# The low-part scores matmul over 128 rows instead of 64, with the low part of k kept twice per head

## The chip, the cores and the metric

The kernel runs on one core of one Trainium2 chip. The metric is the device time of one execution in microseconds (us), from the first to the last instruction of that core. Timed runs are given as a median; the profile is of one separate execution of the same program.

## The reference

Two layers of a block that mixes a latent sequence of 256 tokens with a context of 256 tokens, both of width 1024, all in float32. Each layer has a feed-forward part, a mixer, and a second feed-forward part; the last layer leaves out what only the context would need. The mixer is the part that matters here. It projects to queries, keys and values of 64 per head, and computes

```
s = jnp.einsum('bqhgd,bkhd->bhgqk', qi, k).astype(jnp.float32) * scale
p = jax.nn.softmax(s, axis=-1).astype(v.dtype)
return jnp.einsum('bhgqk,bkhd->bqhgd', p, v)
```

for attention A (6 query heads on 2 key heads, with normed q and k, and rotary positions for the latent tokens) and attention B (6 heads, with a position bias and a window for the latent tokens). Latent queries see 256 latent and 256 context keys, context queries the 256 context keys alone. A short convolution over 256 channels is the third mixer, and the three results are projected by w_o. Width of a head: 64, half of the 128 rows of TensorE's array.

## The kernel before

**Numbers.** Float32 products are made of three matmuls of the type float32r: an operand x is split into a high part h (x cast to float32r) and a low part l = x - h, and x times w is h*wh + l*wh + h*wl. Weights come by DMA into a staging buffer (stg, two of them), ScalarE casts the high part (L93), VectorE subtracts to get the low one (L94), and both stand in one buffer of a ring of eight (name w, each 128x2x1024). All matmuls go through one helper (L79).

**Scores.** Since a head has 64 rows, high and low part of q share one stationary block of 128 rows: for the head of half b (rows R[b], 0 to 63 or 64 to 127), the rows R[b] of the block hold the high part, the other 64 the low one. That is AQ for attention A and BQ for B. The keys' high part stands in both halves (AK, BK), so that one matmul over 128 rows gives qh*kh + ql*kh. The low part of k stands once, in the rows of its own head (AL 128x512 for two heads, BL likewise), so the second matmul runs over 64 rows only, those of qh, and gives qh*kl. `unit` does this for a head and 128 queries:

```
mm(ps, q, k, True, False)
mm(ps, q[R[b]], kl[R[b]], False, True)
```

Behind it come, per unit: VectorE's negative row maximum nmx (L571; with bias, the sum and maximum in one, L574), ScalarE's exponential P with its row sum (L579), VectorE's reciprocal and scaling (L581, L582), two or four transpositions on TensorE (ptr, L586), ScalarE's copy PT (L588). `pair` takes two units (b = 0, 1) and multiplies their PT with V (pv, a stationary block of 64 columns each). The scores take one of two PSUM banks (name at).

**Stages.** `mixer` runs once per layer. In layer 0 (`full`) it has latent and context queries: 24 units of 256 keys and 24 of 512. In layer 1 it has the latent ones alone: 24 units of 512. So there are 72 units. `token_block` projects V, q and k of 128 tokens and fills AQ, AK and AL through a transposition (L471 to L480); `fm_b` projects q and k of attention B and fills BK, BQ and BL (L527 to L533), which lie in ring buffers, four of the eight, until attention B is done; `fm_conv` is the convolution, with six weight units. The output projection needs eight weight units (woa).

**Order.** The code above is traced in program order, and a scheduler then orders each engine's instructions by a model of its own. So ordinary matmuls of the projections and of the output projection stand between the scores, transpositions and pv of the attention. Each engine works its instructions in that order. SyncE's queue issues the DMAs of weights (stg) and of the bias (L606, two bias buffers in layer 0, four in layer 1) in order too: one that waits for its buffer holds up those behind it.

Of the kernel before, what the change touches and what calls it, by code (L numbers as in the profile page):

```python
# [8 lines left out]
F32 = mybir.dt.float32  # L9
F32R = mybir.dt.float32r  # L10
BF16 = mybir.dt.bfloat16
AF = mybir.ActivationFunctionType
ALU = mybir.AluOpType
# [12 lines left out]
def tile_hybrid_block(ctx: ExitStack, tc: tile.TileContext, xin, c2, w_ada, w_ada0, bcol, grow, gcol, win, qkg, bias_in,  # L26
                      convw, woa, wi, wi_tm, wo, ident, rope, out):
    nc = tc.nc
    pe, act, dve, pool, sp = nc.tensor, nc.scalar, nc.vector, nc.gpsimd, nc.sync
# [17 lines left out]
    CW = const.tile([128, 2, 3, 2], F32, name="CW")  # L47
# [30 lines left out]
    def mm(out, lhsT, rhs, first, last):  # L78
        pe.matmul(out, lhsT=lhsT, rhs=rhs, start=first, stop=last)  # L79
# [341 lines left out]
    def mixer(ph, l, U, after):  # L421
# [8 lines left out]
        nq = 512 if full else 256  # L430
        AQ = ph.tile([128, 3, 2, nq], F32R, name="AQ", tag="AQ")
        AK = ph.tile([128, 2, 512], F32R, name="AK", tag="AK")
        AL = ph.tile([128, 512], F32R, name="AL", tag="AL")
        R = [slice(0, 64), slice(64, 128)]

        wv = [load_unit(win[l, j]) for j in range(4)]
# [1 line left out]
        BQ, BK, BL = [], [], []  # L438

        def token_block(t):  # L440
            p = tm_block(U, t, wv)
            act.copy(V[:, t], p)
            h0 = 0 if (full or t < 2) else 6
            nh = 8 - h0
            p = tm_block(U, t, wqk, 64 * h0)
            pv = p.rearrange("p (h d) -> p h d", d=64)[:, h0:8]
            sq = ph.tile([128, 8, 64], F32, name="sq", tag="t2", bufs=4)
            act.activation(sq[:, h0:8], pv, AF.Square)
            ss = small.tile([128, 8], F32, name="ss8", tag="ss8")
            dve.tensor_reduce(out=ss[:, 0:nh], in_=sq[:, h0:8], op=ALU.add, axis=AX.X)  # L450
            r = rstd(ss[:, 0:nh], 64, nh)
            qn = ph.tile([128, 8, 64], F32, name="qn", tag="t2", bufs=4)
            dve.tensor_tensor(out=qn[:, h0:8], in0=pv, in1=r.unsqueeze(2).to_broadcast([128, nh, 64]), op=ALU.mult)
            dve.tensor_tensor(out=qn[:, h0:8], in0=qn[:, h0:8], in1=GT[:, h0:8], op=ALU.mult)
            if t < 2:
                m1 = ph.tile([128, 8, 64], F32, name="m1", tag="t2", bufs=4)
                dve.tensor_tensor(out=m1, in0=qn, in1=ROPE[:, t, 0:1].to_broadcast([128, 8, 64]), op=ALU.mult)
                m2 = sq
                qv = qn.rearrange("p h (a s f) -> p (h a) s f", a=2, s=2)
                mv = m2.rearrange("p h (a s f) -> p (h a) s f", a=2, s=2)  # L460
                sv = ROPE[:, t, 1].rearrange("p (a s f) -> p a s f", a=2, s=2)
                for s in range(2):
                    dve.tensor_tensor(
                        out=mv[:, :, s].rearrange("p (h a) f -> p h a f", a=2),
                        in0=qv[:, :, 1 - s].rearrange("p (h a) f -> p h a f", a=2),
                        in1=sv[:, :, s].unsqueeze(1).to_broadcast([128, 8, 2, 16]), op=ALU.mult)
                dve.tensor_tensor(out=qn, in0=m1, in1=m2, op=ALU.add)
            pt = ps_tr.tile([128, 4, 128], F32, name="ptr", tag="ptr")
            j0 = h0 // 2
            for j in range(j0, 4):  # L470
                pe.transpose(pt[:, j], qn[:, 2 * j:2 * j + 2].rearrange("p h d -> p (h d)"), I)  # L471
            c = slice(128 * t, 128 * t + 128)
            for b in range(2):
                if j0 == 0:
                    act.copy(AQ[R[b], :, b, c], pt[R[b], 0:3])
                    dve.tensor_tensor(out=AQ[R[1 - b], :, b, c], in0=pt[R[b], 0:3],
                                      in1=AQ[R[b], :, b, c].bitcast(F32), op=ALU.subtract)
                act.copy(AK[R[b], b, c], pt[R[b], 3])
                dve.tensor_copy(AK[R[1 - b], b, c], AK[R[b], b, c])
                dve.tensor_tensor(out=AL[R[b], c], in0=pt[R[b], 3], in1=AK[R[b], b, c].bitcast(F32), op=ALU.subtract)  # L480

        def fm_tile(idx, c0, n, w=None):
            w = w or load_unit(win[l, idx])
# [7 lines left out]
            return p  # L491

        oa = work.tile([128, 2, 512], F32, name="uf", tag="uf")
        ob = ph.tile([128, 512], F32, name="ob", tag="ob")
        oc = work.tile([128, 2, 512], F32, name="xn", tag="xn")
        od = work.tile([128, 4, 256], F32, name="grow", tag="grow")
        b0 = 256 if full else 0
# [15 lines left out]
        def fm_b():  # L513
            ws = {8 + x: load_unit(win[l, 8 + x]) for x in (0, 3, 1, 4)}
            bl = []
            for _ in range(4):
                w = next_slot().rearrange("p a (b c) -> p (a b) c", c=512)
                dve.memset(w[0:1, 0, 0:1].bitcast(F32), 0.0)
                bl.extend(w[:, x] for x in range(4))
            for j in range(3):  # L520
                BK.append(bl[2 * j:2 * j + 2])
                BQ.append(bl[6 + 2 * j:8 + 2 * j])
                BL.append(bl[12 + j])
            for j in range(3):
                p = fm_tile(8 + j, 0, 512, ws.get(8 + j))
                for b in range(2):
                    act.copy(BK[j][b][R[b]], p[R[b]])  # L527
                    dve.tensor_copy(BK[j][b][R[1 - b]], BK[j][b][R[b]])
                    dve.tensor_tensor(out=BL[j][R[b]], in0=p[R[b]], in1=BK[j][b][R[b]].bitcast(F32), op=ALU.subtract)
                p = fm_tile(11 + j, 0, nq, ws.get(11 + j))  # L530
                for b in range(2):
                    act.activation(BQ[j][b][R[b], 0:nq], p[R[b], 0:nq], AF.Copy, scale=0.125)
                    dve.scalar_tensor_tensor(out=BQ[j][b][R[1 - b], 0:nq], in0=p[R[b], 0:nq], scalar=0.125,  # L533
                                             in1=BQ[j][b][R[b], 0:nq].bitcast(F32), op0=ALU.mult, op1=ALU.subtract)

        def fm_conv():
            for ct in range(2):
                px = fm_tile(14 + 3 * ct, 0, nq)
                cx = ph.tile([128, 512], F32, name="cx", tag="t2", bufs=4)
                act.copy(cx[:, 0:nq], px[:, 0:nq])  # L540
                pc = fm_tile(15 + 3 * ct, 0, nq)
                ns = nq // 256
                z = ph.tile([128, 2, 258], F32, name="z", tag="z")
                dve.memset(z, 0.0)
                dve.tensor_tensor(out=z[:, 0:ns, 1:257], in0=pc[:, 0:nq].rearrange("p (s t) -> p s t", t=256),
                                  in1=cx[:, 0:nq].rearrange("p (s t) -> p s t", t=256), op=ALU.mult)
                o = oc[:, ct]
                ov = o[:, 0:nq].rearrange("p (s t) -> p s t", t=256)
                dve.tensor_scalar(out=ov, in0=z[:, 0:ns, 0:256], scalar1=CW[:, l, 0, ct:ct + 1], scalar2=None,
                                  op0=ALU.mult)  # L550
                dve.scalar_tensor_tensor(out=ov, in0=z[:, 0:ns, 1:257], scalar=CW[:, l, 1, ct:ct + 1], in1=ov,
                                         op0=ALU.mult, op1=ALU.add)
                dve.scalar_tensor_tensor(out=ov, in0=z[:, 0:ns, 2:258], scalar=CW[:, l, 2, ct:ct + 1], in1=ov,
                                         op0=ALU.mult, op1=ALU.add)
                pb = fm_tile(16 + 3 * ct, 0, nq)
                dve.tensor_tensor(out=o[:, 0:nq], in0=pb[:, 0:nq], in1=o[:, 0:nq], op=ALU.mult)
# [3 lines left out]
        for x in BIAS:  # L560
            pool.memset(x[:, 256:512], 0.0)

        def unit(q, k, kl, b, nk, bias):
            p = bank("at")
            ps = p[:, 0:nk]
            mm(ps, q, k, True, False)
            mm(ps, q[R[b]], kl[R[b]], False, True)
            nmx = small.tile([128, 1], F32, name="nmx", tag="nmx")
            P = ph.tile([128, 512], F32, name="P", tag="P", bufs=3 if full else 4)
            if bias is None:  # L570
# [2 lines left out]
            else:  # L573
                dve.tensor_tensor_reduce(out=P[:, 0:nk], in0=ps, in1=bias, op0=ALU.add, op1=ALU.max, scale=1.0,  # L574
                                         scalar=NEG, accum_out=nmx)
# [15 lines left out]
        def pair(A, j, qt):  # L591
# [3 lines left out]
            for b in range(2):  # L595
                qs = slice(128 * qt, 128 * qt + 128)
                ks = slice(k0, k0 + nk)
                if A:
                    pts.append(unit(AQ[:, j, b, qs], AK[:, b, ks], AL[:, ks], b, nk, None))
                else:  # L600
                    bias = None
                    if lat:
                        h = 2 * j + b
                        bias = BIAS[bn[0] % len(BIAS)]
                        bn[0] += 1
                        (sp).dma_start(out=bias[:, 0:256], in_=bias_in[l, h, qt])  # L606
                    pts.append(unit(BQ[j][b][:, qs], BK[j][b][:, ks], BL[j][:, ks], b, nk, bias))
            pb = bank("pv")
            po = pb[:, 0:128]
            for kb in range(nk // 128):  # L610
# [176 lines left out]
```

## Time and profile before

| what | value |
| --- | --- |
| time, median of 3 runs | 1735.74 us (1734.5 to 1735.75) |
| span of the profiled execution | 1736.0 us |
| TensorE matmul busy | 1706.0 us (98%), 9098 matmuls |
| TensorE weight loads busy | 1412.8 us (81%) |
| VectorE busy | 1201.1 us (69%) |
| ScalarE busy | 704.2 us (41%) |
| GpSimd busy | 52.1 us (3%) |
| TensorE's granted clock, mean | 0.999 of full speed |
| data moved by DMA | 257.31 MB, mean 148 GB/s |

The first mixer's attention lies at about 440 to 610 us of the span, the second's at about 1444 to 1512. In the profile, PE is TensorE's matmuls and PEld its weight loads, DVE is VectorE, ACT ScalarE, POOL GpSimd and SP SyncE. An L with a number is the line of the kernel. A matmul's own duration includes its pipelined end; how long it holds the array is the distance from its start to the start of the next one. "issue" as a releaser means that nothing that the profile shows held the instruction back.

### The profile page before, as it was taken

The numbers are of one execution on the slowest core, as the hardware profiler recorded it, in microseconds if no ns is written. First come the engines' busy times: TensorE is split into PE (matmuls) and PEld (weight loads), VectorE is DVE, ScalarE is ACT, GpSimd is POOL, SyncE is SP. The second block draws the span as 40 slices with busy tenths as digits, with TensorE's granted clock in tenths as the row PEclk, the third lists the DMA queues.
The fourth block names the chain that finished last, engine by engine and source line by source line (L and its number), as shares of the span: only waits on it lengthen the run. The fifth ranks groups of instructions, "written<-read, shape, count | busy, mean of one in ns | idle before, by whom it ended". The sixth has DMA issues, their size and how long they took to land.

```text
span 1736.0 us, 23269 instructions
## 1 busy us (share of the span) xinstructions
PE 1706.0 (98%) x9098; PEld 1412.8 (81%) x9098; DVE 1201.1 (69%) x1721; ACT 704.2 (41%) x1215; POOL 52.1 (3%) x76
## 2 busy tenths in 40 slices
PE   6999999999999999999999999999999999999997
PEld 4888888888777689888888888888888888779997
DVE  3579789877755565576776666888795767766564
ACT  5432222236545564322222264322222646665442
POOL 1000000002000010000000010000000110000000
PEclk9999999999999999999999999999999999999999
DMA  8566555522211134554444234665563323346551
GB/s 311 178 223 199 179 192 189 171 81 96 85 61 49 43 103 156 166 177 152 159 158 147 71 111 167 209 202 187 159 206 111 122 77 110 98 168 220 183 187 68
DMA packets 75613, 257.31 MB, mean 148 GB/s; under 512 B 10976, under 2 KB 14256, under 8 KB 74992
## 3 DMA queue, kind: packets, MB, share of 16 engines
q1 hardware_dynamic: 74304, 250.29, 43.9%
q0 software_dynamic: 1200, 5.55, 0.8%
q8 instruction: 71, 1.16, 0.3%
q14 instruction: 38, 0.31, 0.1%
HBM read 254.71 MB, written 1.09 MB: 147 GB/s over the span
## 4 chain that ended last, share of the span: by engine, by line
PE 94%; DMA 2%; DVE 1%; ACT 1%; issue 1%; SPq 0%; POOL 0%; DVEq 0%; POOLq 0%; ACTq 0%
PE mm L79 50%; PE at L79 26%; PE pv L79 14%; PE ptr L586 2%; PE ptr L234 1%; DMA GT<-in_qkg_dram 1%; DMA stg<-in_wi_tm_dram 1%; DVE w L94 0%; DMA stgx<-in_wo_dram 0%; ACT junk L217 0%; DMA H<-in_xin_dram 0%; ACT xn L229 0%; ACT w L93 0%; PE ptr L79 0%; PE ptr L471 0%
## 5 line engine op out<-in xcount | busy, mean ns | idle before, releaser
L79 PE MATMUL mm<-Uh,w 128*128 128x512 f32 (+1 forms) x1808 | 489.3, 350 | 0.0
L93 ACT CAST w<-stg 128x1024 fp32r<-128x1024 f32 x262 | 274.7, 1050 | 465.9 <-PE mm L79 395.2
L94 DVE TENSOR_TENSOR w<-stg,w 128x1024 fp32r<-128x1024 f32 x262 | 319.2, 1220 | 162.5 <-ACT w L93 161.9
L79 PEld LDWEIGHTS mm<-Uh,w 128*128 128x128 f32 x1808 | 318.8, 189 | 47.0 <-issue 5.4
L79 PE MATMUL mm<-Ul,w 128*128 128x512 f32 (+1 forms) x904 | 316.2, 350 | 0.0
L161 DVE SCALAR_TENSOR_TENSOR acc<-adas,S,acc 128x1024 f32<-128x1024 f32 x217 | 268.8, 1277 | 8.5 <-DMA adas<-in_w_ada_dram 8.0
L79 PE MATMUL at<-Uh,w 128*128 128x512 f32 (+1 forms) x960 | 253.8, 344 | 0.8 <-ACT Uh L272 0.8
L79 PE MATMUL mm<-w,a 128*128 128x512 f32 x924 | 228.1, 390 | 0.0
L79 PEld LDWEIGHTS mm<-w,a 128*128 128x128 f32 x924 | 173.1, 188 | 35.7
L79 PEld LDWEIGHTS mm<-Ul,w 128*128 128x128 f32 x904 | 171.2, 189 | 23.5 <-issue 2.4
L79 PEld LDWEIGHTS at<-Uh,w 128*128 128x128 f32 x960 | 168.8, 190 | 22.6 <-ACT Uh L272 1.3
L79 PE MATMUL mm<-w,Uh 128*128 128x512 f32 (+1 forms) x544 | 172.2, 390 | 0.8 <-ACT w L93 0.8
L79 PE MATMUL at<-Ul,w 128*128 128x512 f32 (+1 forms) x480 | 165.4, 345 | 1.8 <-DVE Ul L273 1.8
L79 PE MATMUL at<-w,a 128*128 128x512 f32 x594 | 147.6, 391 | 0.4 <-ACT a L325 0.4
L79 PEld LDWEIGHTS at<-w,a 128*128 128x128 f32 x594 | 110.8, 188 | 23.7 <-ACT a L325 1.3
L79 PE MATMUL pv<-Uh,w 128*128 128x512 f32 (+1 forms) x464 | 127.7, 352 | 0.0
L79 PEld LDWEIGHTS mm<-w,Uh 128*128 128x128 f32 x544 | 100.1, 188 | 22.2 <-issue 2.2
L94 DVE TENSOR_TENSOR w<-stgx,w 128x1024 fp32r<-128x1024 f32 x58 | 71.0, 1223 | 53.1 <-ACT w L93 52.9
L320 DVE TENSOR_TENSOR sg<-mm,sg 128x512 f32<-128x512 f32 (+1 forms) x86 | 51.1, 594 | 81.6 <-PE mm L79 80.2
L79 PE MATMUL mm<-w,Ul 128*128 128x512 f32 (+1 forms) x272 | 105.7, 389 | 1.5 <-DVE Ul L253 1.5
L79 PEld LDWEIGHTS at<-Ul,w 128*128 128x128 f32 x480 | 91.0, 190 | 13.3 <-DVE Ul L273 2.4
L79 PEld LDWEIGHTS pv<-Uh,w 128*128 128x128 f32 x464 | 82.7, 189 | 12.0
(160 smaller groups left out, 1806.3 us busy)
## 6 DMA issues: line engine op xcount, KB each, us to landing
adas<-in_w_ada_dram SPq DMA_DIRECT2D x144, 512.0 KB, 4.0
stg<-in_wi_dram SPq DMA_DIRECT2D x124, 512.0 KB, 4.2
stg<-in_wo_dram SPq DMA_DIRECT2D x66, 512.0 KB, 3.4
stg<-in_win_dram SPq DMA_DIRECT2D x40, 512.0 KB, 3.3
stgx<-in_wi_dram SPq DMA_DIRECT2D x36, 512.0 KB, 4.2
stgx<-in_wo_dram SPq DMA_DIRECT2D x22, 512.0 KB, 4.3
stg<-in_woa_dram SPq DMA_DIRECT2D x16, 512.0 KB, 3.3
stg<-in_wi_tm_dram SPq DMA_DIRECT2D x16, 512.0 KB, 3.4
```

Source lines behind the costliest of these rows:

```text
L79: pe.matmul(out, lhsT=lhsT, rhs=rhs, start=first, stop=last)
L93: act.copy(w[:, 0], s)
L94: dve.tensor_tensor(out=w[:, 1], in0=s, in1=w[:, 0].bitcast(F32), op=ALU.subtract)
L161: dve.scalar_tensor_tensor(out=acc[:, v], in0=s, scalar=S[:, kt, v:v + 1], in1=acc[:, v], op0=ALU.mult, op1=ALU.add)
L234: pe.transpose(pt[:, b], xn[:, 128 * k:128 * k + 128], I)
L320: dve.tensor_tensor(out=sg[:, 0:n], in0=pss[f, 1][:, 0:n], in1=sg[:, 0:n], op=ALU.mult)
L586: pe.transpose(pt[:, b], P[:, 128 * b:128 * b + 128], I)
```

## The change

AL and BL get a second half: for each head, all 128 rows hold the low part of k. In `token_block` and `fm_b`, ScalarE copies the low part to the other 64 rows after VectorE's subtraction. The second matmul of a unit takes the whole stationary block q, as the first one does, over 128 rows, and so also adds ql*kl. BL of three head pairs takes six slices instead of three, so `fm_b` holds five ring buffers instead of four, dealt out so that those of the first heads come free first. Two tiles are cut to what layer 1 uses of them (ob, z).

```diff
-        AL = ph.tile([128, 512], F32R, name="AL", tag="AL")
+        AL = ph.tile([128, 2, 512], F32R, name="AL", tag="AL")
...
-                dve.tensor_tensor(out=AL[R[b], c], in0=pt[R[b], 3], in1=AK[R[b], b, c].bitcast(F32), op=ALU.subtract)
+                dve.tensor_tensor(out=AL[R[b], b, c], in0=pt[R[b], 3], in1=AK[R[b], b, c].bitcast(F32),
+                                  op=ALU.subtract)
+                act.copy(AL[R[1 - b], b, c], AL[R[b], b, c].bitcast(F32))
...
-        ob = ph.tile([128, 512], F32, name="ob", tag="ob")
+        ob = ph.tile([128, nq], F32, name="ob", tag="ob")
...
-            for _ in range(4):
+            for _ in range(5):
                 w = next_slot().rearrange("p a (b c) -> p (a b) c", c=512)
                 dve.memset(w[0:1, 0, 0:1].bitcast(F32), 0.0)
                 bl.extend(w[:, x] for x in range(4))
-            for j in range(3):
-                BK.append(bl[2 * j:2 * j + 2])
-                BQ.append(bl[6 + 2 * j:8 + 2 * j])
-                BL.append(bl[12 + j])
+            for j, (kq, lo) in enumerate(((0, 4), (8, 6), (12, 16))):
+                BK.append(bl[kq:kq + 2])
+                BQ.append(bl[kq + 2:kq + 4])
+                BL.append(bl[lo:lo + 2])
...
-                    dve.tensor_tensor(out=BL[j][R[b]], in0=p[R[b]], in1=BK[j][b][R[b]].bitcast(F32), op=ALU.subtract)
+                    dve.tensor_tensor(out=BL[j][b][R[b]], in0=p[R[b]], in1=BK[j][b][R[b]].bitcast(F32),
+                                      op=ALU.subtract)
+                    act.copy(BL[j][b][R[1 - b]], BL[j][b][R[b]].bitcast(F32))
...
-                z = ph.tile([128, 2, 258], F32, name="z", tag="z")
+                z = ph.tile([128, ns, 258], F32, name="z", tag="z")
...
-        def unit(q, k, kl, b, nk, bias):
+        def unit(q, k, kl, nk, bias):
             p = bank("at")
             ps = p[:, 0:nk]
             mm(ps, q, k, True, False)
-            mm(ps, q[R[b]], kl[R[b]], False, True)
+            mm(ps, q, kl, False, True)
```

The scheduler's order changes with it. The rows below are the program's instructions in the order of their engine, with line, operation, out<-in and size; four lines were added, so L586 of before is L590, and L606 is L610.

On TensorE, at the first scores of the first mixer, this is the piece of the difference; mm are ordinary projection matmuls:

```order
 L79 MATMUL mm<-w,Uh 128x512 x2
 L79 MATMUL at<-AK,AQ 128x256
+L79 MATMUL mm<-w,Ul 128x512
+L79 MATMUL mm<-w,Uh 128x512 x2
 L79 MATMUL at<-AL,AQ 128x256
 L79 MATMUL mm<-w,Ul 128x512
```

Three ordinary matmuls now stand between the first and the second scores matmul of that unit.

On ScalarE, where the token blocks of the context fill AQ, AK and AL, before:

```order
L478 CAST AK<-ptr 64x128
L475 CAST AQ<-ptr 64x3x128
L478 CAST AK<-ptr 64x128
L475 CAST AQ<-ptr 64x3x128
L478 CAST AK<-ptr 64x128
L448 ACTIVATE sq<-mm 128x512
```

and after:

```order
L478 CAST AK<-ptr 64x128
L482 CAST AL<-AL 64x128
L475 CAST AQ<-ptr 64x3x128
L478 CAST AK<-ptr 64x128
L475 CAST AQ<-ptr 64x3x128
L482 CAST AL<-AL 64x128
L478 CAST AK<-ptr 64x128
L448 ACTIVATE sq<-mm 128x512
```

The copies of AL (L482) stand between the casts of AK and AQ; each waits for VectorE's subtraction.

On SyncE's queue, where the first mixer's weights of the output projection (woa) and the biases of its latent units are loaded, before:

```order
L91 DMA stg<-in_woa_dram 128x1024 x6
L606 DMA bias_3297<-in_bias_dram 128x256
L606 DMA bias_3298<-in_bias_dram 128x256
L606 DMA bias_3297<-in_bias_dram 128x256
L606 DMA bias_3298<-in_bias_dram 128x256
L606 DMA bias_3297<-in_bias_dram 128x256
L606 DMA bias_3298<-in_bias_dram 128x256
L606 DMA bias_3297<-in_bias_dram 128x256
L606 DMA bias_3298<-in_bias_dram 128x256
L91 DMA stg<-in_woa_dram 128x1024
```

and after:

```order
L91 DMA stg<-in_woa_dram 128x1024 x5
L610 DMA bias_3297<-in_bias_dram 128x256
L610 DMA bias_3298<-in_bias_dram 128x256
L610 DMA bias_3297<-in_bias_dram 128x256
L610 DMA bias_3298<-in_bias_dram 128x256
L91 DMA stg<-in_woa_dram 128x1024
L610 DMA bias_3297<-in_bias_dram 128x256
L610 DMA bias_3298<-in_bias_dram 128x256
L610 DMA bias_3297<-in_bias_dram 128x256
L610 DMA bias_3298<-in_bias_dram 128x256
L91 DMA stg<-in_woa_dram 128x1024 x2
```

The sixth woa load stood ahead of all eight of these biases and now stands between them, behind four and ahead of four.

## Rows read from the trace of the kernel before

**Rows 1.** The page, engines: busy us, share of the span, instructions.

```profile
PE 1706.0 (98%) x9098; PEld 1412.8 (81%) x9098; DVE 1201.1 (69%) x1721; ACT 704.2 (41%) x1215; POOL 52.1 (3%) x76
```

**Rows 2.** Waits of PE, 425 to 625 us: who, for whom, us, times, longest.

```profile
PE pv L79 <- ACT PT L588: 0.2, 1, 0.2
```

**Rows 3.** Groups by form on PEld, whole span: busy, mean ns, idle before.

```profile
L79 PEld LDWEIGHTS mm<-w,Uh 128*128 128x128 f32 x544 | 100.1, 188 | 22.2 <-issue 2.2 <-ACT w L93 1.2
...
L79 PEld LDWEIGHTS at<-w 64*128 64x128 f32 x36 | 6.6, 183 | 8.1 <-issue 6.7
L79 PEld LDWEIGHTS at<-AL,AQ 64*128 64x128 f32 x36 | 6.6, 183 | 9.4 <-issue 8.0 <-DVE rs L581 0.6 <-DVE AL L480 0.6
```

**Rows 4.** Timeline of PE, first mixer, 512 keys: start us, us, instruction.

```profile
511.73 0.39 PE L79 MATMUL mm<-Ul,w 128*128 128x512 f32 x1
511.96 0.39 PE L79 MATMUL at<-AK,AQ 128*128 128x512 f32 x1
512.28 0.50 PE L79 MATMUL at<-AL,AQ 64*128 64x512 f32 x1
512.70 0.72 PE L79 MATMUL mm<-Uh,w 128*128 128x512 f32 x2
513.27 0.60 PE L586 MATMUL ptr<-I,P 128*128 128x128 f32 x4
```

**Rows 5.** Timeline of PE: a unit of 256 keys; ordinary matmuls of 256 columns.

```profile
443.77 0.28 PE L79 MATMUL at<-AK,AQ 128*128 128x256 f32 x1
443.98 0.38 PE L79 MATMUL at<-AL,AQ 64*128 64x256 f32 x1
444.29 0.73 PE L79 MATMUL mm<-w,Uh 128*128 128x512 f32 x2
444.86 0.40 PE L79 MATMUL mm<-w,Ul 128*128 128x512 f32 x1
...
1449.35 0.28 PE L79 MATMUL mm<-Ul,w 128*128 128x256 f32 x1
1449.47 0.40 PE L79 MATMUL mm<-Uh,w 128*128 128x256 f32 x2
```

**Rows 6.** Timeline of PE, first mixer, attention B of the latent tokens.

```profile
577.93 0.40 PE L79 MATMUL mm<-w,Uh 128*128 128x512 f32 x1
578.25 0.43 PE L79 MATMUL pv<-PT,V 128*64 128x128 f32 x2
...
578.81 0.90 PE L79 MATMUL at<-w 128*128 128x512 f32 x2
579.64 0.66 PE L586 MATMUL ptr<-I,P 128*128 128x128 f32 x4
```

**Rows 7.** Timeline of PE, second mixer: a unit followed by pv.

```profile
1509.67 0.81 PE L79 MATMUL at<-w 128*128 128x512 f32 x2
1510.41 0.77 PE L79 MATMUL pv<-PT,V 128*64 128x128 f32 x10
```

**Rows 8.** Timeline, attention B of the context; in brackets idle time and releaser.

```profile
561.95 0.42 PEld L79 LDWEIGHTS pv<-PT,V 128*64 128x64 f32 x8 [0.17 <-ACT PT L588]
...
562.54 0.50 PEld L79 LDWEIGHTS at<-w 128*128 128x128 f32 x2 [0.17 <-ACT PT L588]
...
564.32 0.20 PEld L586 LDWEIGHTS ptr<-I,P 128*128 128x128 f32 x2 [0.17 <-DVE P L582]
...
567.05 0.67 PE L79 MATMUL at<-w 128*128 128x256 f32 x2
```

**Rows 9.** Chain that ended last, 588 to 595 us: start, us, what.

```profile
590.80 2.76 DMA bias<-in_bias_dram
```

**Rows 10.** Groups by form on ACT, 425 to 625 us: busy, mean ns, idle before.

```profile
L93 ACT CAST w<-stg 128x1024 fp32r<-128x1024 f32 x20 | 20.7, 1048 | 2.3 <-DMA stg<-in_woa_dram 1.6 <-PE mm L79 0.5
...
L527 ACT CAST w<-mm 64x512 fp32r<-64x512 f32 x6 | 3.5, 580 | 4.1 <-PE mm L79 4.0
```

**Rows 11.** The same on DVE.

```profile
L94 DVE TENSOR_TENSOR w<-stg,w 128x1024 fp32r<-128x1024 f32 x20 | 24.3, 1219 | 6.8 <-ACT w L93 6.6
```

More of the change, by code (lines that the diff above doesn't have):

```diff
@@ L542, in fm_conv @@
                 ns = nq // 256
-                z = ph.tile([128, 2, 258], F32, name="z", tag="z")
+                z = ph.tile([128, ns, 258], F32, name="z", tag="z")
                 dve.memset(z, 0.0)
-                dve.tensor_tensor(out=z[:, 0:ns, 1:257], in0=pc[:, 0:nq].rearrange("p (s t) -> p s t", t=256),
+                dve.tensor_tensor(out=z[:, :, 1:257], in0=pc[:, 0:nq].rearrange("p (s t) -> p s t", t=256),
                                   in1=cx[:, 0:nq].rearrange("p (s t) -> p s t", t=256), op=ALU.mult)
@@ L548, in fm_conv @@
                 ov = o[:, 0:nq].rearrange("p (s t) -> p s t", t=256)
-                dve.tensor_scalar(out=ov, in0=z[:, 0:ns, 0:256], scalar1=CW[:, l, 0, ct:ct + 1], scalar2=None,
+                dve.tensor_scalar(out=ov, in0=z[:, :, 0:256], scalar1=CW[:, l, 0, ct:ct + 1], scalar2=None,
                                   op0=ALU.mult)
-                dve.scalar_tensor_tensor(out=ov, in0=z[:, 0:ns, 1:257], scalar=CW[:, l, 1, ct:ct + 1], in1=ov,
+                dve.scalar_tensor_tensor(out=ov, in0=z[:, :, 1:257], scalar=CW[:, l, 1, ct:ct + 1], in1=ov,
                                          op0=ALU.mult, op1=ALU.add)
-                dve.scalar_tensor_tensor(out=ov, in0=z[:, 0:ns, 2:258], scalar=CW[:, l, 2, ct:ct + 1], in1=ov,
+                dve.scalar_tensor_tensor(out=ov, in0=z[:, :, 2:258], scalar=CW[:, l, 2, ct:ct + 1], in1=ov,
                                          op0=ALU.mult, op1=ALU.add)
@@ L598, in pair @@
                 if A:
-                    pts.append(unit(AQ[:, j, b, qs], AK[:, b, ks], AL[:, ks], b, nk, None))
+                    pts.append(unit(AQ[:, j, b, qs], AK[:, b, ks], AL[:, b, ks], nk, None))
                 else:
@@ L606, in pair @@
                         (sp).dma_start(out=bias[:, 0:256], in_=bias_in[l, h, qt])
-                    pts.append(unit(BQ[j][b][:, qs], BK[j][b][:, ks], BL[j][:, ks], b, nk, bias))
+                    pts.append(unit(BQ[j][b][:, qs], BK[j][b][:, ks], BL[j][b][:, ks], nk, bias))
             pb = bank("pv")
```

## The prediction

> **What bounds the kernel now.** The table of engines comes first: TensorE is busy for 98% of the span [rows 1]. A busy matmul is not yet one at full pace, since the ends of pipelined matmuls are modelled, so two more things are needed: whether TensorE waits for anybody, and how far apart its matmuls start. The first is in the waits of the first mixer, 425 to 625 us: TensorE's matmuls waited for another engine once, 0.2 us [rows 2]; over the second mixer's attention (1430 to 1512 us) that view is empty. So in both mixers, the only place that the change touches, time is what the matmul stream itself takes. The second is in the weight loads by form: the 72 loads of 64 rows (two groups of 36) had their port idle before them for 9.4 + 8.1 = 17.5 us, 0.24 us each; for 544 full loads of the ordinary stream it is 22.2 us, 0.04 each [rows 3]. The load itself is no shorter for having half the rows (183 against 188 ns). A full load runs while the matmul before it streams; a 64-row load starts only afterwards. How much that costs must be read from starts, not from durations.
>
> **What the 64-row matmul costs.** An ordinary stream of 512 columns starts a matmul every 0.227 us: 511.73 to 511.96 [rows 4]. There the first scores matmul starts at 511.96, the 64-row one 0.32 later at 512.28, the next matmul 0.42 after that at 512.70, and that one and its successor take 0.57 until 513.27. So these four take 1.31 us, where four at the ordinary pace would take 0.91: **0.40 us lost**. It is lost three times: before the 64-row load, after it (the following full load is not taken early either), and a last 0.11 in the matmul after that. With 256 columns [rows 5]: 443.77 to 444.86 is 1.09 us for two matmuls of 256 columns and two of 512; at the ordinary pace of 0.12 (1449.35 to 1449.47) and 0.227 it would be 0.69, so **0.40** again.
>
> Not all of it goes away. Loads of 64 columns (the matmuls of the probabilities with V) are late as well, and stay so: an ordinary matmul followed by one takes 0.32 instead of 0.227 (577.93 to 578.25) [rows 6]. A pair followed by that takes 0.74 (1509.67 to 1510.41) [rows 7] and would take 0.227 + 0.32 = 0.55: 0.19 saved. A pair between two groups of transpositions takes 0.83 (578.81 to 579.64) [rows 6]; of this the 0.09 by which it is longer than 0.32 + 0.42 comes from the transpositions ahead and stays, so 0.55 is left and 0.28 is saved.
>
> **The sum of the gain.** Counted in the program's order before, of the 72 pairs 48 are followed by another full load, 13 by a 64-column load and 11 by transpositions (in the changed order 50, 12 and 10, so the new order itself moves this by a few tenths): 48 x 0.40 + 13 x 0.19 + 11 x 0.28 = 19.2 + 2.5 + 3.1 = **24.8 us**. The ends are 72 x 0.19 = 13.7 and 72 x 0.40 = 28.8. The step rests on the new second matmul behaving as any full one. It is the pattern that the stream already has: two matmuls in a row with the same full stationary block (w with Uh, then w with Ul) start 0.227 apart.
>
> The trace shows a full load running during a matmul on the same rows. The Trainium skill ("TensorE: Matmul & The Clock Gate", Part 3, The mechanism) says that a load overlaps a running matmul only when their row groups differ. By that sentence a full second load would be as late as the 64-row one and the sum would be nil. The trace disagrees for full loads (0.04 us idle) and agrees for 64-row ones (0.24 us); I let the trace decide and keep the rule as a rival.
>
> **What the change adds.** ScalarE gets 28 casts: 12 of 64x512 for BL, like the BK cast of 0.58 us [rows 10], and 16 of 64x128 for AL, which can't take longer. That is at most 28 x 0.58 = 16 us of ScalarE time over both mixers. TensorE waits for next to none of ScalarE's work there [rows 2], so I take 0; uncovered, they would cost those 16. The AL casts lie behind a VectorE subtraction and ahead of the first scores, and ScalarE's next casts of AQ and AK queue behind them; there the new order puts three ordinary matmuls (0.7 us) between first and second scores matmul, which covers one cast. VectorE gets as many operations as before; the smaller memset of z is worth tenths.
>
> The scores' keys and queries now hold five ring buffers of eight until attention B ends, so three instead of four carry weights. A weight must be cast and subtracted (1.05 + 1.22 us) [rows 10, 11] between the last matmul that read its buffer and its first use. While three carry the stream, TensorE works 24 matmuls (24 x 0.227 = 5.4 us, or 24 x 0.12 = 2.9 in the second mixer) on each of the other two, so 5.8 us or more are there for 2.3: I take 0. On SyncE's queue the sixth woa load still stands ahead of four bias loads, but now it waits for the staging buffer of the fourth, which is emptied only when the first heads of attention B let a ring buffer go. These biases queue behind it; who waits for them is VectorE's sum of scores and bias, then the scores two units on. That chain is late already once, where a bias takes 2.76 us [rows 9]. I charge 1 us for this, about what the three pairs right behind that bias lose now and may not get back.
>
> **What is late next.** In the B units of the context tokens the pairs come with few ordinary matmuls between, and loads are already released by ScalarE and VectorE, not by the stream: 561.95 and 562.54 by ScalarE's PT copy, 564.32 by VectorE's P [rows 8]. From 562.54 to 567.05 four such units pass [rows 8], 1.13 us each, at the pace of those two engines. A faster TensorE only waits there. At that pace eight units lie between 560 and 569 us, and 8 x 0.28 = 2.2 us of the gain is given back. Together with the 1 us above: **3.2 us**.
>
> **Result of the sum:** 24.8 - 3.2 = 21.6 us off. The profiled execution's span is 1736.0 us and the median of the timed runs 1735.74, the same to 0.02%, so nothing is to be scaled: 1735.74 - 21.6 = **1714 us**.
>
> **Rivals.**
> - *The data chain takes the bound.* TensorE's matmuls get shorter, but nmx, exponential, reciprocal, P and the PT copy form a chain per unit that does not; wherever few ordinary matmuls stand between, the gain turns into waits. For it: the releases of 561 to 565 us. Against it: elsewhere in the mixers TensorE waits for none. If all 24 B units of the first mixer gave back theirs (24 x 0.4 = 9.6), 1735.7 - 24.8 + 9.6 = 1721.
> - *No change.* By the skill's rule or for another reason the second load stays late: the copies cost nothing and the gain is nil, 1736. Against it: the ordinary stream's full loads.
> - *Slower: weights starve.* Three ring buffers are too few: ScalarE's cast stands at a buffer not yet free, and the exponentials queue behind it. In each mixer eight units pass through the three (two of fm_b's late tiles and six of the convolution); if each showed the whole 2.27 us, 16 x 2.27 = 36 us, and the time would be 1735.7 - 21.6 + 36 = 1750. It decides from 21.6 / 16 = 1.35 us per unit on. Against it: the 20 weight casts of the first mixer had ScalarE idle for 2.3 us in all, most of it for DMA [rows 10].
>
> **How the numbers follow.** Forecast (gain of 13 to 29, little given back) 0.86; data chain 0.07; no change 0.04; starving 0.03. A difference under 0.2%, 3.5 us, can't be told from none by the runs shown. Faster: 0.86 + 0.07 = 0.93; same 0.04; slower 0.03. The range goes from 1735.7 - 28.8 = 1707, rounded up to 1708 since all 72 pairs at the best price is the very end, to the data chain's 1721, and 1 more: 1722. The 13.7 us end with nothing given back also lies at 1722.
>
> **What would show it.** In the profile after: the second loads as 128x128 with the idle time before them near 0.04 us each; a pair of 512 columns amid others taking 0.45 from first start to the next; the first mixer some 14 to 16 us shorter and the second 6 to 8, with nothing changed in the feed-forward parts. Given back: waits of TensorE's loads for ScalarE's PT or exponential around the B units of the context. The forecast is wrong if the second load still waits, if loads wait for the weight cast, or if bias loads show up in the chain several times.

## The result: 18 us faster, and where the rest of the gain stayed

The changed kernel takes **1717.28 us** (median of 4 runs, 1717.20 to 1719.36) against 1735.51 for the kernel before (4 runs, 1734.50 to 1735.75): a ratio of 0.9899, interval 0.9885 to 0.9913. The forecast was 1714, with 1708 to 1722 as the range. Measured again later (after_again below) it took 1716.42 against 1735.23 (0.9892, interval 0.9877 to 0.9906).

The page of the profile after: span, engines, and the chain that ended last by engine.

```profile
span 1715.4 us, 23300 instructions
...
PE 1684.8 (98%) x9098; PEld 1413.9 (82%) x9098; DVE 1200.1 (70%) x1723; ACT 715.0 (42%) x1243; POOL 49.0 (3%) x76
...
PE 96%; DMA 1%; DVE 1%; ACT 1%; issue 0%; POOL 0%; SPq 0%; DVEq 0%; POOLq 0%; ACTq 0%
```

Beside [rows 1]: TensorE's busy time fell by 21.2 us (1706.0 to 1684.8), ScalarE's rose by 10.8 with 28 instructions more, and TensorE still bounds the kernel (96% of the chain, 94% before).

The same trace's weight loads by form (busy, mean ns of one, idle time just before), beside [rows 3]:

```profile
L79 PEld LDWEIGHTS at<-w 128*128 128x128 f32 x72 | 11.6, 189 | 3.0 <-DVE nmx L578 0.6 <-DVE nmx L580 0.5 <-issue 0.5
...
L79 PEld LDWEIGHTS at<-AL,AQ 128*128 128x128 f32 x36 | 6.8, 190 | 0.7
```

There are no loads of 64 rows any more. The 36 second loads of attention A have 0.7 us idle before them, 0.02 each, where they had 9.4; those of attention B now stand in one group with the first loads, 72 with 3.0 us, 0.04 each.

A unit of 512 keys amid other matmuls, timeline of TensorE after (start us, us, instruction), beside [rows 4]:

```profile
499.74 0.39 PE L79 MATMUL at<-AK,AQ 128*128 128x512 f32 x1
499.97 0.39 PE L79 MATMUL mm<-Ul,w 128*128 128x512 f32 x1
500.20 0.39 PE L79 MATMUL at<-AL,AQ 128*128 128x512 f32 x1
500.42 0.62 PE L79 MATMUL mm<-Uh,w 128*128 128x512 f32 x2
```

Every step is 0.22 to 0.23 us: the pair of scores matmuls runs at the pace of the ordinary stream.

**Where the time went.** Both kernels run 9098 matmuls, so the n-th of one trace can be set against the n-th of the other. The table gives the difference in start (kernel minus the profiled run of before), as the change over five stretches: up to the first mixer (matmul 2100, 416.1 us in the trace before), the first mixer (to 3300, 644.5), the feed-forward parts and loads between (to 7190, 1433.4), the second mixer to its last pv matmuls (to 7818, 1529.9), and from there into the last feed-forward part (to 8010, 1568.3). Where an order differs inside a mixer a border is good to some tenths, and in x7_tail_early, whose order differs most at the border of the last two stretches, only their sum counts (-5.0, as in x4_tail_order); behind 8010 nothing moves by more than 0.03 in any kernel. The kernels whose names begin with x are those of the experiments below.

| us against before | to the mixer | first mixer | between | second mixer | its end | all |
|---|---|---|---|---|---|---|
| after | +0.2 | -17.1 | -1.2 | -7.5 | **+4.9** | -20.7 |
| x1_copies_only | -0.5 | +0.2 | -0.8 | -1.4 | **+6.0** | +3.5 |
| x6_copies_tail | -1.9 | +0.1 | -1.4 | -1.6 | +2.7 | -2.0 |
| x2_shared_low | -0.6 | -17.2 | -1.2 | -7.9 | -1.0 | -27.9 |
| x3_lat_only | -0.5 | -7.6 | -1.1 | -7.9 | -1.0 | -18.0 |
| x4_tail_order | -0.5 | -17.1 | -1.1 | -7.8 | +2.8 | -23.7 |
| x4_again | -0.3 | -17.1 | -1.4 | -7.8 | +2.3 | -24.2 |
| x7_tail_early | -1.3 | -17.1 | -1.0 | -9.3 | +4.3 | -24.4 |
| x5_shared_tail | -0.7 | -13.7 | -0.1 | -8.4 | +1.1 | -21.8 |
| after_again | -0.1 | -17.1 | -0.9 | -7.5 | **+6.6** | -19.1 |

The mixers give 24.6 us. Then, at the end of the second mixer, 4.9 come back as a loss. The third column looks like a property of the profiled run of before, since all kernels but x5_shared_tail show it, also those that change nothing there. The same may go for some of the fourth: x1 and x6, which keep the 64 rows, stand at -1.4 and -1.6 in it. Against these two the changed kernel's mixers gain 17.2 and 6.0, 23.2 us.

**The place of the loss.** The waits of TensorE in the changed kernel from 1500 to 1530 us (who, line, for whom, us, times, longest):

```profile
PE at L79 <- ACT Uh L252: 3.8, 1, 3.8
PE at L79 <- DVE Ul L253: 1.7, 1, 1.7
```

The same stretch in its timeline of TensorE (in brackets idle time and what ended it):

```profile
1509.67 0.40 PE L79 MATMUL mm<-w,Uh 128*128 128x512 f32 x1
1509.90 1.04 PE L234 MATMUL ptr<-I,xn 128*128 128x128 f32 x8
1514.75 0.79 PE L79 MATMUL at<-w,Uh 128*128 128x512 f32 x1 [3.81 <-ACT Uh L252]
...
1517.62 0.80 PE L79 MATMUL at<-w,Ul 128*128 128x512 f32 x1 [1.66 <-DVE Ul L253]
1518.22 1.06 PE L79 MATMUL at<-w,Uh 128*128 128x512 f32 x2
1519.07 0.63 PE L79 MATMUL at<-w,Ul 128*128 128x512 f32 x1
```

and the corresponding rows of the kernel before:

```profile
1531.39 1.09 PE L234 MATMUL ptr<-I,xn 128*128 128x128 f32 x8 [0.45 <-ACT xn L229]
1532.24 0.71 PE L79 MATMUL mm<-w,Uh 128*128 128x512 f32 x2
...
1536.43 0.39 PE L79 MATMUL at<-w,Uh 128*128 128x512 f32 x1
```

The last feed-forward part begins with eight transpositions of xn (ptr<-I,xn); ScalarE and VectorE turn them into uf, Uh and Ul, and only then can the first feed-forward matmul (at<-w,Uh) run. Before, projection matmuls of the mixer from 1532.24 to 1536.43, 4.2 us, stood between and covered that. In the changed kernel the scheduler put the transpositions behind the last projection matmul, so TensorE stands still. That sets off a second loss, in the granted clock. By stretches of 10 us of the changed kernel (length, busy time and instructions of PE, PEld, DVE, ACT and POOL, then the mean granted clock, DMA share, GB/s):

```profile
1500.00:1510.00 10.00, 10.00 (x53) 7.44 (x52) 6.83 (x10) 6.80 (x13) 2.19 (x2) 1.00 0.39 122
1510.00:1520.00 10.00, 4.54 (x17) 3.11 (x16) 8.14 (x14) 7.40 (x15) 1.67 (x3) 0.72 0.60 210
```

After a standstill of 3.8 us the clock is at its lower level, 1.2 GHz: the two matmuls from 1518.22 to 1519.07 take 0.43 us each instead of 0.23.

### The profile page after: what moved, and what is told of

It reads as the page before. It is cut to its first block, busy times and chain, and to the rows that moved or that the text cites. A ratio compares the mean times of both kernels' runs of the same rounds, so it can differ in the third digit from the quotient of the medians.

```text
span 1715.4 us, 23300 instructions
## 1 busy us (share of the span) xinstructions
PE 1684.8 (98%) x9098; PEld 1413.9 (82%) x9098; DVE 1200.1 (70%) x1723; ACT 715.0 (42%) x1243; POOL 49.0 (3%) x76
## 4 chain that ended last, share of the span: by engine, by line
PE 96%; DMA 1%; DVE 1%; ACT 1%; issue 0%; POOL 0%; SPq 0%; DVEq 0%; POOLq 0%; ACTq 0%
PE mm L79 51%; PE at L79 27%; PE pv L79 15%; PE ptr L590 2%; PE ptr L234 1%; DMA GT<-in_qkg_dram 1%; DMA H<-in_xin_dram 0%; DMA stg<-in_wi_tm_dram 0%; DVE H L280 0%; DVE w L94 0%; ACT junk L217 0%; PE ptr L79 0%; PE ptr L471 0%; PE ptr L386 0%; ACT xn L229 0%
## 5 line engine op out<-in xcount | busy, mean ns | idle before, releaser
L79 PEld LDWEIGHTS at<-Uh,w 128*128 128x128 f32 x960 | 168.9, 190 | 22.6 <-ACT Uh L272 0.9
L79 PEld LDWEIGHTS at<-w,a 128*128 128x128 f32 x594 | 110.8, 188 | 23.2 <-ACT a L325 0.8
```

## The experiments

**The additions without the wide matmul.** The changed kernel, with

```
-            mm(ps, q, kl, False, True)
+            mm(ps, q[R[b]], kl[R[b]], False, True)
```

> All that the change adds (28 ScalarE copies of the low part, five ring buffers held instead of four, the narrower ob and z), while the second scores matmul runs over 64 rows as before, reading only the half that it read before. Same output as before. Theory (additions are hidden): 1735.5 us as before, within 0.2%, 1732 to 1739, with the 64-row loads idle 0.24 us each before them. Rival (the additions cost about 4 us, and this is why 25 us of gain became 18): 1738 to 1741. Rival (starving weights): above 1745.

Measured: 1740.33 us (1739.62 to 1741.41, 6 runs) against 1734.58 for before; ratio 1.0031, interval 1.0019 to 1.0043. The first rival's number: the additions cost 5.7 us. But the table shows where. In the first mixer, with 14 of the 28 copies and the fifth buffer, they cost 0.2 us. The whole loss is at the end of the second mixer, with the waits of the changed kernel (x1_copies_only, 1510 to 1550 us):

```profile
PE at L79 <- ACT Uh L252: 4.0, 1, 4.0
PE at L79 <- DVE Ul L253: 1.5, 1, 1.5
```

There the transpositions of xn stand behind the last projection matmul too. So not the work of the copies but the order that came with them is the suspect, and it came without the wide matmul.

**The wide matmul without the additions.** The kernel before, with

```
-            mm(ps, q[R[b]], kl[R[b]], False, True)
+            mm(ps, q, kl, False, True)
```

> The kernel before with one thing changed: the second scores matmul runs over all 128 rows of the AL or BL that both heads share, with no copies and four ring buffers. It therefore adds, on the other 64 rows, the low part of q times the low part of the other head's k, which is of the size of rounding and is not in the reference's sum. Theory: the whole gain is the width of the second matmul, 24.8 us, and the loss at the start of the last feed-forward part (6.2 us in the changed kernel, of which about 2 came back) comes from the place of the transpositions of xn in the order, which here stand ahead of the last projection matmuls as in the kernel before: 1710 to 1712 us. Rival (the loss belongs to any kernel whose TensorE gets there 25 us early, since the weight DMA and ScalarE are then behind): about 1716 to 1718, as the changed kernel.

Measured: 1711.59 us (1709.19 to 1714.19, 4 runs) against 1734.58, ratio 0.9867 (0.9850 to 0.9884). Here the transpositions stand where they stood before, 18 projection matmuls ahead of the first feed-forward matmul, and TensorE's waits from 1490 to 1530 us are

```profile
PE at L79 <- ACT Uh L252: 0.9, 1, 0.9
...
```

The loss at the end is gone (-1.0 in the table), with TensorE arriving there 27 us early. The rival (whoever comes early waits there) falls.

**The order alone, on the changed kernel.** The transposition is remembered when it is recorded, and part of the last projection group is held behind it:

```
+                late = not full and (t, hf) == (1, 1) and k >= 4
+                with tc.issue_after(last_tr[0].ins) if late else nullcontext():
                     mm(p, O[0][:, k, c], wh, k == 0, False)
                     mm(p, O[1][:, k, c], wh, False, False)
                     mm(p, O[0][:, k, c], wl, False, k == 7)
```

> The changed kernel, with the last 12 matmuls of the second mixer's last projection group held behind the transpositions of the first xn tile of the last feed-forward part, so that they cover the copies and subtractions that make Uh and Ul. Same computation. Theory (order costs the 3.8 and 1.7 us that TensorE waits there for Uh and Ul, and the 6.8 us of half clock behind it): 1712 to 1714 us, the two waits under 1 us, granted clock full between 1500 and 1530 us. Rival (ScalarE's in-order cast of the weight staged at 1505.7 to 1510.2 us is what holds Uh back): 1716 to 1718, the wait for Uh stays above 2 us.

Measured: 1713.65 us (1711.59 to 1714.46, 4 runs) against 1734.58, ratio 0.9873 (0.9858 to 0.9888), inside the theory's 1712 to 1714.

> The changed kernel on the chip and in the call of x4_again. 1717 us, as at first; the waits for Uh and Ul at the start of the last feed-forward part are there again, 3.8 and 1.7 us, with the half clock behind them.

> The kernel of x4_tail_order beside the changed kernel on one chip. Theory (the order of the transpositions is worth the 3 us that the two traces differ by): 3 to 4 us under after_again, 1713 to 1714. Rival (the difference between two calls was that of two chips): within 1 us of after_again.

Measured side by side on one chip: after_again 1716.42 us (1714.22 to 1718.83), x4_again 1713.36 (1711.93 to 1715.52), 4 runs each; 3.1 us apart, where the first measurements, made apart, gave 3.6. The ranges touch and the intervals of the ratios (0.9877 to 0.9906, and 0.9858 to 0.9891) overlap, so by the times alone the gain is likely rather than settled; the traces show it at its place. Waits of TensorE from 1490 to 1540 us, after_again first, x4_again below:

```profile
PE at L79 <- ACT Uh L252: 4.4, 1, 4.4
PE at L79 <- DVE Ul L253: 1.7, 1, 1.7
```

```profile
PE at L79 <- ACT Uh L254: 1.3, 1, 1.3
PE ptr L388 <- ACT uf L250: 1.2, 1, 1.2
PE mm L79 <- ACT Uh L514: 0.7, 1, 0.7
PE at L79 <- DVE Ul L255: 0.6, 1, 0.6
```

and x4_again's clock stays at its upper level (same columns as above):

```profile
1510.00:1520.00 10.00, 8.06 (x35) 6.03 (x34) 7.97 (x11) 6.65 (x14) 1.18 (x2) 1.00 0.78 268
```

The wait for Uh was expected under 1 us and stayed at 1.3 to 1.7, so of the rival's cause something is left: ScalarE takes its work in order, and ahead of uf and Uh it holds weight casts, one of which waits for its transfer. ScalarE in the changed kernel:

```profile
1510.21 1.05 ACT L93 CAST w<-stg 128x1024 fp32r<-128x1024 f32 x1 [1.18 <-DMA stg<-in_wi_tm_dram]
...
1511.75 1.50 ACT L248 ACTIVATE uf<-ptr,COLS,GP 128x128 f32<-128x128 f32 x4
1513.12 1.06 ACT L93 CAST w<-stg 128x1024 fp32r<-128x1024 f32 x1
1514.05 1.16 ACT L252 CAST Uh<-uf 128x512 fp32r<-128x512 f32 x2
```

In x4_again a weight cast of 1.05 us still stands between the two casts of Uh (1511.20), without a wait.

**More cover.** The same edge with `k >= 1` in place of `k >= 4`.

> The changed kernel, with 21 instead of the 12 matmuls of x4_tail_order held behind the transpositions of xn, about as many as in the kernel before (20). Same computation. Theory (x4 still waits 1.7 us for Uh and 0.6 us for Ul because twelve matmuls, 2.7 us, cover too little): both waits under 0.3 us, 1711 to 1713 us, 1 to 2 us under x4. Rival (the transpositions then wait for xn, as 0.4 us in x2_shared_low): no better than x4, 1713 to 1715.

Measured: 1714.14 us (1713.00 to 1715.12, 4 runs) against 1735.48, ratio 0.9878 (0.9863 to 0.9893): no better than x4, so this theory fell. The kernel before has 18 matmuls there and not 20. Waits of TensorE from 1490 to 1530 us, and below them ScalarE's cast ahead of those of Uh:

```profile
PE at L79 <- ACT Uh L254: 1.6, 2, 0.9
...
PE ptr L236 <- ACT xn L231: 0.8, 1, 0.8
```

```profile
1510.91 1.05 ACT L93 CAST w<-stg 128x1024 fp32r<-128x1024 f32 x1 [1.63 <-DMA stg<-in_wi_tm_dram]
```

The transpositions come 1.2 us sooner (1506.42 against 1507.64) and wait for xn, and the first Uh matmul starts at 1513.05 against 1513.18: here ScalarE stands 1.63 us for the transfer of a weight whose cast comes ahead of those of Uh, so with enough cover, by this trace, it is that which sets the start, as the rival of x4_tail_order had it. In x2_shared_low the same place waits 0.34 us. By the traces x2_shared_low is 3.5 to 4.0 us better than x4 and x7 over the last two stretches of the table, by the times about 2; what makes up the rest of that wasn't separated.

**The order on the kernel with 64 rows.** x1_copies_only with the edge of x4_tail_order.

> The kernel of x1_copies_only (copies and five buffers, second matmul over 64 rows; 1740.3 us) with the order edge of x4_tail_order: the last 12 projection matmuls stand behind the transpositions of xn. Same computation as before. Theory (of the 5.7 us that x1 lost, the place of the transpositions is all but nothing): 1736 to 1738 us, the wait for Uh under 2 us, full clock there. Rival (the copies or the held buffers cost it): 1740 as x1.

Measured: 1737.13 us (1735.93 to 1738.31, 10 runs) against 1735.48, ratio 1.0010 (1.0000 to 1.0019). So of x1's 5.7 us the order took 4.1, and the additions are left with 1.7, at the edge of what can be told from none. The wait for Uh stayed at 2.7 us where under 2 were expected, with a clock of 0.83 behind it, so not all of the order's cost is gone in this kernel either.

**The price by kind of unit.** x2_shared_low for the units with 512 keys alone:

```
+            if nk == 512:
+                mm(ps, q, kl, False, True)
+            else:
+                mm(ps, q[R[b]], kl[R[b]], False, True)
```

> The kernel of x2_shared_low (1711.6 us), but only for the 48 units with 512 keys; the 24 units of the context with 256 keys keep the 64-row second matmul of the kernel before. In the wide units the low part of q times the low part of the other head's k is added. Theory (every pair is worth 0.4 us, the context units too): 24 x 0.40 = 9.6 us less gain than x2, 1720 to 1722. Rival (the step of the prediction by which the context's B units are paced by ScalarE and VectorE and give their gain back): 7.4 us less at most, 1718 to 1719.

Measured: 1719.60 us (1717.71 to 1720.86, 4 runs) against 1735.48, ratio 0.9909 (0.9894 to 0.9924). The median stands 8.0 us above x2's, 7.1 if each is set against the kernel before beside it: between the two theories, or nearer the rival. The traces tell them apart. In the first mixer, where the 24 units lie, x3 gains 7.6 and x2 17.2: 9.6 us, a mean of 0.40 for each of the 24, and the second mixer is the same to 0.1. Over the last 11 pairs of the context's B units both kernels have the same order on TensorE, so there each pair can be priced by itself. One that stands ahead of transpositions, x2 first, x3 below:

```profile
550.19 0.51 PE L79 MATMUL at<-w 128*128 128x256 f32 x2
...
550.88 0.43 PE L79 MATMUL pv<-PT,V 128*64 128x128 f32 x2
```

```profile
558.02 0.70 PE L79 MATMUL at<-w 128*128 128x256 f32 x2
...
559.01 0.43 PE L79 MATMUL pv<-PT,V 128*64 128x128 f32 x2
```

From its start to pv it takes 0.69 in place of 0.99 us. The pairs that stand alone give 0.30 to 0.34 ahead of transpositions, 0.15 to 0.19 ahead of pv and 0.38 to 0.39 ahead of ordinary matmuls, close to the prediction's own prices (0.28, 0.19, 0.40), and all 11 together 3.3 us, 0.30 each. So the B units give nothing back; the other 13 pairs gave 6.3 us, 0.48 each, where the orders differ, and that the mean of all is 0.40 is partly chance.

**What makes a load late.** Two kernels of matmul streams alone.

> Nothing of the reference is computed: ten streams of matmuls of 512 (two of 256) columns into two alternating PSUM banks, 32 each behind a warm-up of 64. All full; full and rows 0 to 63 in turn; full and rows 64 to 127 in turn; all rows 0 to 63; rows 0 to 63 and 64 to 127 in turn; full and rows 0 to 31 in turn; full and full with 64 columns of weights in turn; with 256 columns, all full and full/64 rows in turn. Theory (a load that does not fill the array cannot run during the matmul before it, a full one can): all full 0.23 us a matmul; each mixed pair of full and 64 rows 0.80 to 0.85 us, whichever half; all 64 rows about 0.40 each; full and 32 rows as with 64; full and 64 columns 0.55 a pair; with 256 columns 0.12 each and 0.50 to 0.65 a pair. Rival (the change of row group between neighbours costs it, not the size of the load): all 64 rows 0.23 each, and only the mixed ones slow. Rival (two different row groups can overlap): rows 0 to 63 and 64 to 127 in turn at 0.23 or less each.

> Nothing of the reference is computed: seven short streams, each right behind 40 full matmuls that bring TensorE to its full clock. Rows 0 to 63 alone; full and rows 64 to 127 in turn; rows 0 to 63 and 64 to 127 in turn; two full, then two of rows 0 to 63, in turn; three full, then one as the kernel's probabilities with V (exact float32, 64 columns of weights, 128 streamed), in turn; the same with 128 columns of weights; the same with 64 columns but in the fast float type. Theory now, from m1_loads (a load is late when its rows are neither the same as those of the running matmul nor apart from them; a row range of 64 alone is not late): rows 0 to 63 alone 0.227 us a matmul; full and rows 64 to 127 in turn 0.43 each; rows 0 to 63 and 64 to 127 in turn 0.23 for a pair of two; two and two 1.31 for the four, as one pair in the kernel (one change to 64 rows and one back lose 0.40 together). For the last three: if the 0.09 us ahead of a matmul with V comes from its 64 columns, the first and third show it; if from its number type, the first and second. Rival (64 rows are late whatever runs before them): 0.43 each for rows 0 to 63 alone at full clock, and 1.7 for two and two.

These two compute other things than the kernel and were run once each. m1_loads gave, by the starts in its trace: all full 0.227 us a matmul; full and rows 0 to 63 in turn 0.43 each at full clock, full and rows 0 to 31 also 0.43; full and full with 64 columns of weights 0.23 each, where 0.55 a pair was expected; with 256 columns 0.12 and 0.31. But rows 0 to 63 alone took 0.427 at half clock, just what a full stream takes at half clock: not late at all. So the theory (a load that does not fill the array is late) fell, and the first rival held; so did the second, with 0.43 for a pair of rows 0 to 63 and 64 to 127 at half clock. Since the clock had fallen to half in the stream before and stayed there, m2_loads repeats it with 40 full matmuls ahead of each stream. Its timeline of weight loads (idle time before in brackets): rows 0 to 63 alone; full and rows 64 to 127 in turn; rows 0 to 63 and 64 to 127 in turn; two and two; three full and one like the kernel's pv; the same with full exact float32; the same with 64 columns of the fast type.

```profile
17.01 3.52 PEld L58 LDWEIGHTS onelo<-A,W 64*128 64x128 f32 x16 [0.35 <-issue]
...
31.25 0.18 PEld L58 LDWEIGHTS althi<-A,W 64*128 64x128 f32 x1 [0.25 <-issue]
...
50.59 1.68 PEld L58 LDWEIGHTS lohi<-A,W 64*128 64x128 f32 x16 [0.35 <-issue]
...
63.05 0.30 PEld L58 LDWEIGHTS pairlo<-A,W 128*128 128x128 f32 x2 [0.36 <-issue]
...
77.01 0.19 PEld L58 LDWEIGHTS faltpv<-PT,V 128*64 128x64 f32 x2 [0.35 <-issue]
77.38 0.53 PEld L58 LDWEIGHTS altpv<-A,W 128*128 128x128 f32 x3 [0.17 <-issue]
...
90.80 0.41 PEld L58 LDWEIGHTS faltwide<-PT,V 128*128 128x128 f32 x2
...
103.56 0.13 PEld L58 LDWEIGHTS faltcol<-A,W 128*64 128x64 f32 x1
```

At full clock, rows 0 to 63 alone run at 0.227 us a matmul, like full ones. Full and rows 64 to 127 in turn take 0.43 each. Two of rows 0 to 63 with two full take 1.32 for the four, so one change from all rows to a part of them and back costs 0.41, with one matmul between as with two, and the load at each such change is late (0.36 us idle here). Rows 0 to 63 and rows 64 to 127 in turn run in pairs, 0.23 us for two matmuls that start 0.00 to 0.01 apart, so a change between rows that lie apart costs nothing. Whether the late load comes from rows shared in part or from the change in their number was not separated: no stream changes, say, from 64 rows to 32 others. The lateness ahead of the matmuls with V needs both of its traits: 0.32 before exact float32 with 64 columns, but 0.23 before exact float32 with 128 columns and before 64 columns of the fast type. Neither answer that was expected of the last three is right.

**Both edits.** x2_shared_low with the edge of x4_tail_order.

> The kernel of x2_shared_low (128 rows of the shared low part, no copies, with the low part of q times the other head's low part added) with the order edge of x4_tail_order. Theory: x2 already has the transpositions early, so the edge gives nothing, 1710 to 1712 us, within 1.5 us of x2. Rival (the loss is there whatever the order): as x2 then, about 1716 to 1718, and the edge gives 4 us if x2 has the waits of the changed kernel.

Measured: 1711.74 us (1710.35 to 1716.01, 4 runs) against 1734.58, ratio 0.9868 (0.9853 to 0.9884): the same as x2, as the theory said, though the edge leaves 12 matmuls of cover where x2 had 18, and in the profiled run TensorE waits up to 1.6 us for Uh in place of 0.9. That run shows something else, in the chain and the waits of TensorE from 575 us on:

```profile
574.73 3.86 DMA bias<-in_bias_dram
```

```profile
PE at L79 <- DVE nmx L576: 2.1, 1, 2.1
```

A bias load that took 3.86 us stopped the scores, and the clock was at 0.60 from 580 to 584 us; that run, at 1716.01 us the slowest of the four, lost 3.5 us in the first mixer (13.7 gained in place of 17.2). No other profiled run of a changed kernel has it.

**The best version.** Of the kernels that keep the change's sum, x4_tail_order is the lowest, 1713.4 to 1713.7 us in two measurements against 1716.4 and 1717.3; x7_tail_early (1714.1) can't be told from it. x2_shared_low is at 1711.6 with neither the copies nor the fifth buffer, if the product of the low part of q with the other head's low part is admitted.

## Why the prediction came out, step by step

- **What bounds it: right.** The mixers are TensorE's stream before and after. From 425 to 612 us after, TensorE's matmuls waited once, 0.4 us for VectorE's nmx, beside [rows 2].
- **0.40 us a pair, 24.8 us in all: right.** The mixers gave 24.6 us against the profiled run of before (17.1 and 7.5; 14 to 16 and 6 to 8 were named, so the first gave a little more) and 23.2 against x1 and x6. x3 bore out the three prices pair by pair, and m2 showed 0.41 for a change from all rows to half of them and back. The nearest pair is x4 against x6, the same additions and edge with the wide matmul and without: 20.9 us under the kernel before beside it and 1.7 over, 22.6 us.
- **The reason given for it: incomplete.** The prediction said that a full load runs during the matmul before it and a 64-row one does not. m1 and m2 show that it is the load at a change between all rows and a part of them that is late, not the 64-row load as such. For this kernel the two say the same, since every 64-row matmul stood among full ones. The rule weighed in the prediction (the Trainium skill, "TensorE: Matmul & The Clock Gate", Part 3, The mechanism: a load overlaps a running matmul only when the row groups differ) holds for rows 0 to 63 beside rows 64 to 127 in m2_loads, and does not for a load on the same rows, which was on time both with 128 rows and with 64. Between full matmuls and 64 rows, whose row groups differ but share rows, the load was late (0.24 us), so "differ" can only mean that no row is shared.
- **The copies and the fifth buffer at nothing: right for their work.** ScalarE got 10.8 us more of it (at most 16 said), and the first mixer with all additions and 64 rows (x1, x6) is 0.1 to 0.2 us from before. By the times x6 is still 1.7 us over the kernel before, with a wait of 2.7 us for Uh left at the end.
- **2.2 us given back in the context's B units: wrong.** Next to nothing was. The step read the 0.17 us ahead of the loads in [rows 8], ended by ScalarE's or VectorE's semaphore, as those engines' pace. The same 0.17 stands with no releaser in the kernel before, a little later, and in the changed kernel:

```profile
565.70 0.20 PEld L586 LDWEIGHTS ptr<-I,P 128*128 128x128 f32 x2 [0.17 <-issue]
```

```profile
552.76 0.30 PEld L79 LDWEIGHTS at<-w 128*128 128x128 f32 x2 [0.21 <-ACT P L583]
...
554.46 0.20 PEld L590 LDWEIGHTS ptr<-I,P 128*128 128x128 f32 x2 [0.17 <-issue]
```

  m2_loads has it too (the altpv load at 77.38), where no other engine takes part. So it is a gap that goes with that change of kind of matmul, and a semaphore named beside it is no proof of a wait. The changed kernel's loads do wait for ScalarE's exponential there at one place (552.76 and 553.22, 0.21 and 0.16 us), under 0.4 us in all. Four units took 3.8 us (550.89 to 554.65), 0.94 each with 16 pv matmuls among them, where the step held 1.13, with 10, to be the pace of ScalarE and VectorE.
- **1 us for the bias loads: not there** in the changed kernel's profile, whose chain from 425 to 612 us has no transfer. The mechanism exists, as x5's profiled run shows, in one execution and without the fifth buffer.
- **What was missing: the order outside the mixers.** "The new order itself moves this by a few tenths" was worked out for the neighbours of the 72 pairs and not for what comes after them. The order of the changed kernel shows the transpositions behind the last projection matmul; read against TensorE's chain there, it would have given the copies and subtractions that were covered before and are bare now. The prediction put nothing there. This term is 4.9 to 6.6 us by the traces; the edge gives back 3.1 to 4.1 of it by the times.
- **The base: 1.8 us off.** The prediction held span and time to be the same. In the runs with both, the time is 1.8 us above the span (1717.20 and 1715.4); of 29 later runs of the kernel before, the spans lie between 1731.7 and 1736.0 with a median of 1733.5. The profiled run with 1736.0 was as long as the longest. This is why 20.7 us by the traces are 18.2 by the times.

So 24.8 was right, 3.2 given back was near the 4.9 that came back, but at another place and for another reason: the total within 3.3 us owes something to chance. The rivals: no data chain took the bound, the rule's no change did not happen, and weights did not starve.

## What to carry to other kernels

Count the changes between all rows and a part of them in a matmul stream, not the narrow matmuls: each excursion from 128 rows to 64 and back cost 0.40 us amid ordinary matmuls here, for one matmul or two, and less where the neighbours' loads are late anyway. Look in the changed order at the first work behind the edited part as well: a scheduler can put a producer behind the work that covered its latency, and here that took back a fifth of the gain until an order edge returned part of it. A releaser beside an idle time of a fixed size is no proof of a wait.

## What the runs showed of the hardware

Two matmuls on rows 0 to 63 and rows 64 to 127 start together: 16 of them took 2.1 us in m2_loads where 16 on the same rows took 3.9. At 2.4 GHz a change between 128 rows and 64 costs 0.20 us, at 1.2 GHz 0.30: full and rows 64 to 127 in turn took 0.43 and 0.72 each, where full ones take 0.23 and 0.43. And a stream without a wait for anybody can still lose the clock: full and rows 64 to 127 in turn began at 2.4 GHz in m2_loads and ended at 1.2 within its 8.1 us. It need not: full and rows 0 to 63 in turn, with the same 0.43 us a matmul, kept 2.4 GHz in m1_loads from its start at 32.04 to its end 12.5 us later. What decides it stays open. By stretches, m2_loads first, m1_loads below (length, busy time and instructions of PE, PEld, ACT and POOL, then the granted clock, DMA share, GB/s):

```profile
30.00:33.50 3.50, 3.50 (x11) 1.45 (x9) 0.58 (x1) 0.00 (x0) 1.00 0.00 0
34.00:38.90 4.90, 4.90 (x7) 1.86 (x7) 0.54 (x1) 0.00 (x0) 0.50 0.00 0
```

```profile
40.00:45.00 5.00, 5.00 (x12) 2.05 (x12) 0.28 (x1) 0.00 (x0) 1.00 0.00 0
```
